# Contrast adjustment on one core: 32 KB rows in twelve equal tiles, six buffers, two hardware DMA queues, sums shared by two engines, a first tile loaded in four interleaved pieces, and instructions in program order

## The chip, the cores and the metric

The kernel runs on one core of one Trainium2 chip. The profile's names for its engines are used throughout: DVE (vector work, here the sums and the min), ACT (here the relu and, after the change, half of the sums), PE (matrix products, here to turn the sums of the rows into the images' means), POOL and SP (here they issue DMAs; POOL also writes constants). Sixteen DMA engines (so the page counts them) carry the data between main memory and the on-chip memory; a load is a DMA into the chip, a store one out of it, and each is carried as packets, here one row of a tile each (32 KB on a full tile). A row of a tile lies in one partition of the on-chip memory, a tile in 128 of them (128x8192 in the profile). A buffer is room there for one tile.

The metric is device time in microseconds (us), median of several runs; lower is better. The profile's span, from the first to the last instruction, is a little shorter than the device time: for the same run it is 1.7 to 2.1 us shorter, so differences in span and in time mean the same. Different chips were used for different sets of runs, and each set has its own runs of the kernel before. I compare within a set.

## The reference

```python
batch, c, h, w = 16, 3, 512, 512          # float32, 50.33 MB in, 50.33 MB out
mean = np.mean(x, axis=(2, 3), keepdims=True)
return np.clip(mean + factor * (x - mean), 0, 1)      # factor = 1.5
```

There are 48 images of 512 x 512. Each image needs its whole mean before any of its pixels can be written.

## The kernel before

The kernel writes `factor * x + (1 - factor) * mean`, cut off at 0 by the relu and at 1 by the min. A tile holds four images as 128 rows of 8192 numbers (32 rows per image); the last four images are two tiles of half the size.

```python
TILE_IMGS = [4] * 11 + [2, 2]
X_BUFS = 5
STORE_ENGINE = "gpsimd"
# ... cut: blockw, a block matrix of (1 - factor) / n_pix, one block per image ...
for i, N in enumerate(TILE_IMGS):
    # ... cut: tile and addresses ...
    nc.sync.dma_start(out=xt, in_=src)                     # load, SP's queue
    rsum = rpool.tile([P, 1], f32)
    nc.vector.tensor_reduce(out=rsum, in_=xt, axis=mybir.AxisListType.X, op=mybir.AluOpType.add)
    pbias = psum.tile([P, 1], f32)
    nc.tensor.matmul(pbias, blockw[N], rsum, start=True, stop=True)
    bias = bpool.tile([P, 1], f32)
    nc.scalar.copy(out=bias, in_=pbias)
    nc.scalar.activation(out=xt, in_=xt, func=mybir.ActivationFunctionType.Relu,
                         bias=bias, scale=factor)
    nc.vector.tensor_scalar(out=xt, in0=xt, scalar1=1.0, scalar2=None, op0=mybir.AluOpType.min)
    store_eng.dma_start(out=dst, in_=xt)                   # store, POOL's queue
    # ... cut ...
```

The program does not fix the order of instructions on an engine: the framework's scheduler chooses it.

Of the kernel before, what the change touches and what calls it, by code (L numbers as in the profile page):

```python
# [1 line left out]

# [4 lines left out]


TILE_IMGS = [4] * 11 + [2, 2]  # L10
X_BUFS = 5
STORE_ENGINE = "gpsimd"


@with_exitstack
def kernel(
    ctx: ExitStack,
    tc: tile.TileContext,
    x: bass.AP,
    factor: float,  # L20
    out: bass.AP,
):
    nc = tc.nc
    P = 128

    B, C, H, W = x.shape
    n_img = B * C
    n_pix = H * W

    factor = float(factor)  # L30
    f32 = mybir.dt.float32

    assert sum(TILE_IMGS) == n_img
    NMAX = max(TILE_IMGS)

    x_f = x.rearrange("b c h w -> (b c h w)")
    out_f = out.rearrange("b c h w -> (b c h w)")

    wconst = (1.0 - factor) / float(n_pix)

    consts = ctx.enter_context(tc.tile_pool(name="consts", bufs=1))
    blockw = {}
    for N in sorted(set(TILE_IMGS)):
        wt = consts.tile([P, P], f32, name=f"blockw{N}")
        PPI = P // N
        if N == 1:
            nc.gpsimd.memset(wt, wconst)
        else:
            nc.gpsimd.memset(wt, 0.0)  # L49
            for b in range(N):  # L50
                nc.gpsimd.memset(wt[b * PPI : (b + 1) * PPI, b * PPI : (b + 1) * PPI], wconst)  # L51
        blockw[N] = wt

    xpool = ctx.enter_context(tc.tile_pool(name="xpool", bufs=X_BUFS))
    rpool = ctx.enter_context(tc.tile_pool(name="rpool", bufs=12))
    bpool = ctx.enter_context(tc.tile_pool(name="bpool", bufs=12))
    psum = ctx.enter_context(tc.tile_pool(name="psum", bufs=8, space=bass.MemoryType.PSUM))

    if STORE_ENGINE == "sync":
        store_eng = nc.sync  # L60
    elif STORE_ENGINE == "act":
        store_eng = nc.scalar
    else:
        store_eng = nc.gpsimd

    pix_off = 0
    for i, N in enumerate(TILE_IMGS):
        FREE = n_pix * N // P
        npix_tile = n_pix * N

        xt = xpool.tile([P, NMAX * n_pix // P], f32, name="xt")[:, :FREE]
        src = bass.AP(tensor=x_f.tensor, offset=pix_off, ap=[[FREE, P], [1, FREE]])
        dst = bass.AP(tensor=out_f.tensor, offset=pix_off, ap=[[FREE, P], [1, FREE]])
        nc.sync.dma_start(out=xt, in_=src)  # L74

        rsum = rpool.tile([P, 1], f32)
        nc.vector.tensor_reduce(  # L77
            out=rsum,
            in_=xt,
            axis=mybir.AxisListType.X,  # L80
            op=mybir.AluOpType.add,
        )

        pbias = psum.tile([P, 1], f32)
        nc.tensor.matmul(pbias, blockw[N], rsum, start=True, stop=True)  # L85

        bias = bpool.tile([P, 1], f32)
        nc.scalar.copy(out=bias, in_=pbias)  # L88

        nc.scalar.activation(  # L90
            out=xt,
            in_=xt,
            func=mybir.ActivationFunctionType.Relu,
            bias=bias,
            scale=factor,
        )
        nc.vector.tensor_scalar(  # L97
            out=xt,
            in0=xt,
            scalar1=1.0,  # L100
            scalar2=None,
            op0=mybir.AluOpType.min,
        )
        store_eng.dma_start(out=dst, in_=xt)  # L104

        pix_off += npix_tile


# [1 line left out]
_INS = ['x', 'factor']  # L110
_OUTS = [((16, 3, 512, 512), 'float32')]
#: Inputs that are plain numbers.
_NUMBERS = {'factor': 1.5}


# [26 lines left out]
```

## Time and profile before

| | before |
|---|---|
| time, median of 3 runs | 239.89 us (239.85 to 240.51) |
| span of the profiled run | 238.6 us |
| DVE / ACT busy | 66% / 37% of the span |
| DMA slices at 90% or more | 38 of 40 |

These are lines of the page of the kernel before: busy time per engine, then the span in 40 equal slices (DMA in tenths busy, where 9 is 90% or more, and GB/s moved).

```profile
PE 7.4 (3%) x26; PEld 6.5 (3%) x26; DVE 156.5 (66%) x26; ACT 89.1 (37%) x27; POOL 10.3 (4%) x25
...
DMA  7999999999999999999999999999999999999995
GB/s 269 434 439 439 439 439 352 439 434 439 439 439 439 439 434 434 423 428 412 423 439 439 434 439 439 439 439 439 434 428 426 426 404 428 431 434 439 428 434 214
```

The row of nines is the answer to what bounds the kernel. The packets in the trace say how tight the bound is: a packet of 32 KB takes 1.213 us (median on both queues), and each of the 16 engines carries 100.66 MB / 16 / 32768 = 192 of them, so, at that packet time, 192 x 1.213 = 232.9 us of the 238.6 us cannot be saved by any ordering of this traffic. The other 5.7 us are the start, the end and a few slow packets.

The table of instruction groups, with shapes kept apart, gives the price of each step on a full tile (after the bar: busy us in total, mean ns of one; then the idle time before, and what ended it):

```profile
L77 DVE TENSOR_REDUCE rsum<-xt 128x1 f32<-128x8192 f32 x11 | 95.5, 8685 | 56.1 <-DMA xt<-in_x_dram 56.1
L90 ACT ACTIVATE xt<-xt,bias 128x8192 f32<-128x8192 f32 x11 | 78.4, 7124 | 0.4
L97 DVE TENSOR_SCALAR xt<-xt 128x8192 f32<-128x8192 f32 x11 | 48.6, 4417 | 0.0
```

Finally some lines of the timeline (start, length, engine, line, operation; in brackets the idle time before):

```profile
22.64 7.12 ACT L90 ACTIVATE xt<-xt,bias 128x8192 f32<-128x8192 f32 x1
22.73 8.69 DVE L77 TENSOR_REDUCE rsum<-xt 128x1 f32<-128x8192 f32 x1 [1.02 <-DMA xt<-in_x_dram]
31.33 4.42 DVE L97 TENSOR_SCALAR xt<-xt 128x8192 f32<-128x8192 f32 x1
...
35.66 8.68 DVE L77 TENSOR_REDUCE rsum<-xt 128x1 f32<-128x8192 f32 x1
36.06 0.67 POOL L104 DMA_DIRECT2D out_dram<-xt  x1 [34.02 <-DVE xt L97]
...
205.31 2.46 POOL L104 DMA_DIRECT2D out_dram<-xt  x1 [9.72 <-DVE xt L97]
205.36 2.29 DVE L97 TENSOR_SCALAR xt<-xt 128x4096 f32<-128x4096 f32 x1 [0.34 <-ACT xt L90]
```

DVE sums one tile (22.73) while ACT applies the bias of the one before (22.64), and takes the min of that earlier tile at 31.33. So from one sum to the next DVE needs 35.66 - 22.73 = 12.9 us when nothing is waited for, although a single tile's chain from landed load to issued store lasts 36.06 - 13.0 = 23 us. I call the first number the pitch and the second the chain. (The line at 205.31 is an exception: POOL's issue took 2.46 us instead of 0.53, ending 0.12 us after the DVE instruction that ran from 205.36 to 207.65. It cost nothing here: the packets of that store had their turn only at 216.2 us.) The DMA engines need 19.4 us per tile (2 x 8 packets of 1.213 us per engine), so they, not the pitch, set the pace.

### The profile page before, as it was taken

What the parts mean: (1) busy time and instruction counts of PE and PEld (TensorE: products, weight loads), DVE (VectorE), ACT (ScalarE), POOL (GpSimd) and SP (SyncE); (2) the same over time, 40 slices, a digit from 0 to 9 for tenths busy, and PEclk for the clock granted to TensorE, in tenths of its full rate; (3) what the DMA queues carried; (4) which work ended last, traced back from release to release, by engine and by line L of the source; (5) the groups of instructions that cost most, each with busy time, mean ns of one, the idle gap of its engine ahead of it and who ended that gap; (6) DMA issues with size and microseconds to landing.
All of it is one profiled execution on the core that took longest, in us unless ns stands there. A gap on an engine that the chain in (4) does not pass through costs nothing.

```text
span 238.6 us, 238 instructions
## 1 busy us (share of the span) xinstructions
PE 7.4 (3%) x26; PEld 6.5 (3%) x26; DVE 156.5 (66%) x26; ACT 89.1 (37%) x27; POOL 10.3 (4%) x25
## 2 busy tenths in 40 slices
PE   0000000000000000000000000000000000000000
PEld 0000000000000000000000000000000000000000
DVE  0088999999599079459629909917945979742300
ACT  2002966472906601900920650470190095406000
POOL 2000001000000000000000000000000000500000
DMA  7999999999999999999999999999999999999995
GB/s 269 434 439 439 439 439 352 439 434 439 439 439 439 439 434 434 423 428 412 423 439 439 434 439 439 439 439 439 434 428 426 426 404 428 431 434 439 428 434 214
DMA packets 3744, 100.66 MB, mean 422 GB/s; under 512 B 416, under 2 KB 416, under 8 KB 416
## 3 DMA queue, kind: packets, MB, share of 16 engines
q1 hardware_dynamic: 1872, 50.33, 49.4%
q0 software_dynamic: 1872, 50.33, 49.0%
HBM read 50.33 MB, written 50.33 MB: 422 GB/s over the span
## 4 chain that ended last, share of the span: by engine, by line
issue 38%; DMA 35%; DVE 18%; POOL 2%; POOLq 0%; SPq 0%
DMA xt<-in_x_dram 19%; DMA out_dram<-xt 16%; DVE rsum L77 11%; DVE xt L97 7%; POOL out_dram L104 2%; POOLq L137 0%; SPq L74 0%; POOLq L104 0%
## 5 line engine op out<-in xcount | busy, mean ns | idle before, releaser
L77 DVE TENSOR_REDUCE rsum<-xt 128x1 f32<-128x8192 f32 (+1 forms) x13 | 104.4, 8029 | 61.7 <-DMA xt<-in_x_dram 61.7
L90 ACT ACTIVATE xt<-xt,bias 128x8192 f32<-128x8192 f32 (+1 forms) x13 | 85.8, 6598 | 0.4
L97 DVE TENSOR_SCALAR xt<-xt 128x8192 f32<-128x8192 f32 (+1 forms) x13 | 53.2, 4091 | 5.0 <-ACT xt L90 5.0
L88 ACT COPY bias<-pbias 128x1 f32<-128x1 f32 x13 | 2.1, 160 | 130.6 <-PE pbias L85 130.6
L104 POOL DMA_DIRECT2D out_dram<-xt x13 | 9.0, 692 | 213.0 <-DVE xt L97 212.8
L85 PE MATMUL pbias<-rsum,blockw 128*128 128x1 f32 x26 | 7.4, 355 | 209.5 <-DVE rsum L77 209.5
L85 PEld LDWEIGHTS pbias<-rsum,blockw 128*128 128x128 f32 x26 | 6.5, 311 | 210.3 <-DVE rsum L77 107.1
L88 ACT ACT_TABLE_LOAD x1 | 1.3, 1283 | 0.8 <-PEq L123 0.8
L51 POOL MEMSET blockw<- 32x32 f32 (+1 forms) x6 | 0.8, 128 | 0.2
L49 POOL MEMSET blockw<- 128x128 f32 x2 | 0.3, 205 | 0.3 <-POOLq L123 0.3
L123 POOL MEMSET const-float32-0.0<- 128x1 f32 x1 | 0.1, 104 | 0.2 <-issue 0.2
L123 POOL MEMSET const-bfloat16-1.0<- 128x1 bf16 x1 | 0.1, 113 | 0.0
L123 POOL MEMSET const-uint8-127<- 128x1 uint8 x1 | 0.1, 113 | 0.0
L123 POOL MEMSET const-float32-1.0<- 128x1 f32 x1 | 0.1, 110 | 0.0
## 6 DMA issues: line engine op xcount, KB each, us to landing
xt<-in_x_dram SPq DMA_DIRECT2D x11, 4096.0 KB, 24.6
out_dram<-xt POOLq DMA_DIRECT2D x11, 4096.0 KB, 36.0
xt<-in_x_dram SPq DMA_DIRECT2D x2, 2048.0 KB, 19.5
out_dram<-xt POOLq DMA_DIRECT2D x2, 2048.0 KB, 19.1
```

The source lines that it names most:

```text
L49: nc.gpsimd.memset(wt, 0.0)
L51: nc.gpsimd.memset(wt[b * PPI : (b + 1) * PPI, b * PPI : (b + 1) * PPI], wconst)
L77: nc.vector.tensor_reduce(out=rsum, in_=xt, axis=mybir.AxisListType.X, op=mybir.AluOpType.add,)
L85: nc.tensor.matmul(pbias, blockw[N], rsum, start=True, stop=True)
L88: nc.scalar.copy(out=bias, in_=pbias)
L90: nc.scalar.activation(out=xt, in_=xt, func=mybir.ActivationFunctionType.Relu, bias=bias, scale=factor,)
L97: nc.vector.tensor_scalar(out=xt, in0=xt, scalar1=1.0, scalar2=None, op0=mybir.AluOpType.min,)
L104: store_eng.dma_start(out=dst, in_=xt)
L123: nc = _bacc.Bacc("TRN2", target_bir_lowering=False, num_devices=1)
```

## The change

The intent: rows of 32 KB in every tile, a shorter chain (sums shared by DVE and ACT, relu and min in four overlapping quarters), more buffers, stores from ACT's hardware queue in place of POOL's software queue (hardware_dynamic and software_dynamic on the pages), and an earlier start by loading the first tile in four pieces. The whole diff rewrites the file; this is its core.

```diff
-TILE_IMGS = [4] * 11 + [2, 2]
-X_BUFS = 5
-STORE_ENGINE = "gpsimd"
+P, ROW, BUFS, CHUNK, HALF, JUNK, SPLIT = 128, 8192, 6, 2048, ROW // 2, 2048, 4   # (one per line)
 ...
+    def load(t):
+        xt = xpool.tile([P, ROW], f32, name="xt")
+        if t == 0:
+            for r in range(SPLIT):
+                src = bass.AP(tensor=x_f.tensor, offset=r * ROW,
+                              ap=[[SPLIT * ROW, P // SPLIT], [1, ROW]])
+                nc.sync.dma_start(out=xt[r::SPLIT, :], in_=src)
+        else:
+            nc.sync.dma_start(out=xt, in_=dram(x_f, t))
 ...
+    def compute(t):
-        nc.vector.tensor_reduce(out=rsum, in_=xt, ...)
+        nc.vector.tensor_reduce(out=sums[:, 0:1], in_=xt[:, 0:HALF], ...)
+        for j in range(n_act):                         # (ROW - HALF) // JUNK = 2
+            nc.scalar.activation(out=junk, in_=xt[:, a : a + JUNK], func=Act.Copy,
+                                 accum_out=sums[:, 1 + j : 2 + j])
-        nc.tensor.matmul(pbias, blockw[N], rsum, start=True, stop=True)
+        for j in range(1 + n_act):
+            nc.tensor.matmul(pbias, blockw, sums[:, j : j + 1], start=j == 0, stop=j == n_act)
         nc.scalar.copy(out=bias, in_=pbias)
+        for c in range(0, ROW, CHUNK):
+            nc.scalar.activation(out=part, in_=part, func=Act.Relu, bias=bias, scale=factor)
+            nc.vector.tensor_scalar(out=part, in0=part, scalar1=1.0, scalar2=None, op0=Alu.min)
-        store_eng.dma_start(out=dst, in_=xt)           # gpsimd
+        nc.scalar.dma_start(out=dram(out_f, t), in_=tiles.pop(t))
 ...
+    with tc.manual_schedule():                         # instructions stay in program order
+        for t in range(min(BUFS, n_tiles)):
+            load(t)
+        for t in range(n_tiles):
+            compute(t); store(t)
+            if t + BUFS < n_tiles:
+                load(t + BUFS)
```

(Lines are joined, some are left out, and remarks after # are added for print.) The last block takes the order of instructions out of the scheduler's hands.

More of the change, by code (lines that the diff above doesn't have):

```diff
@@ L5 @@
 import concourse.tile as tile
-from concourse import bass_utils, mybir
+from concourse import mybir
 from concourse._compat import with_exitstack
-TILE_IMGS = [4] * 11 + [2, 2]
-X_BUFS = 5
-STORE_ENGINE = "gpsimd"
+P = 128
+ROW = 8192
+BUFS = 6
+CHUNK = 2048
+HALF = ROW // 2
+JUNK = 2048
+SPLIT = 4
 @with_exitstack
@@ L23 @@
     nc = tc.nc
-    P = 128
+    f32 = mybir.dt.float32
+    Alu = mybir.AluOpType
+    Act = mybir.ActivationFunctionType
     B, C, H, W = x.shape
-    n_img = B * C
-    n_pix = H * W
+    n_img, n_pix = B * C, H * W
+    ppi = n_pix // ROW
+    per_tile = P // ppi
+    n_tiles = n_img // per_tile
+    assert ppi * ROW == n_pix and per_tile * n_tiles == n_img
     factor = float(factor)
-    f32 = mybir.dt.float32
-    assert sum(TILE_IMGS) == n_img
-    NMAX = max(TILE_IMGS)
+    wconst = (1.0 - factor) / float(n_pix)
@@ L36, with dram @@
     x_f = x.rearrange("b c h w -> (b c h w)")
     out_f = out.rearrange("b c h w -> (b c h w)")
-    wconst = (1.0 - factor) / float(n_pix)
+    def dram(ap, t):
+        return bass.AP(tensor=ap.tensor, offset=t * P * ROW, ap=[[ROW, P], [1, ROW]])
     consts = ctx.enter_context(tc.tile_pool(name="consts", bufs=1))
-    blockw = {}
-    for N in sorted(set(TILE_IMGS)):
-        wt = consts.tile([P, P], f32, name=f"blockw{N}")
-        PPI = P // N
-        if N == 1:
-            nc.gpsimd.memset(wt, wconst)
-        else:
-            nc.gpsimd.memset(wt, 0.0)
-            for b in range(N):
-                nc.gpsimd.memset(wt[b * PPI : (b + 1) * PPI, b * PPI : (b + 1) * PPI], wconst)
-        blockw[N] = wt
@@ L54 @@
-    xpool = ctx.enter_context(tc.tile_pool(name="xpool", bufs=X_BUFS))
-    rpool = ctx.enter_context(tc.tile_pool(name="rpool", bufs=12))
-    bpool = ctx.enter_context(tc.tile_pool(name="bpool", bufs=12))
-    psum = ctx.enter_context(tc.tile_pool(name="psum", bufs=8, space=bass.MemoryType.PSUM))
-    if STORE_ENGINE == "sync":
-        store_eng = nc.sync
-    elif STORE_ENGINE == "act":
-        store_eng = nc.scalar
-    else:
-        store_eng = nc.gpsimd
-    pix_off = 0
-    for i, N in enumerate(TILE_IMGS):
-        FREE = n_pix * N // P
-        npix_tile = n_pix * N
-        xt = xpool.tile([P, NMAX * n_pix // P], f32, name="xt")[:, :FREE]
-        src = bass.AP(tensor=x_f.tensor, offset=pix_off, ap=[[FREE, P], [1, FREE]])
-        dst = bass.AP(tensor=out_f.tensor, offset=pix_off, ap=[[FREE, P], [1, FREE]])
-        nc.sync.dma_start(out=xt, in_=src)
-        rsum = rpool.tile([P, 1], f32)
+    xpool = ctx.enter_context(tc.tile_pool(name="xpool", bufs=BUFS))
@@ new lines @@
+    jpool = ctx.enter_context(tc.tile_pool(name="jpool", bufs=1))
+    rpool = ctx.enter_context(tc.tile_pool(name="rpool", bufs=2))
+    bpool = ctx.enter_context(tc.tile_pool(name="bpool", bufs=2))
+    psum = ctx.enter_context(tc.tile_pool(name="psum", bufs=2, space=bass.MemoryType.PSUM))
+    blockw = consts.tile([P, P], f32, name="blockw")
+    nc.gpsimd.memset(blockw, 0.0)
+    for a in range(0, P, ppi):
+        nc.gpsimd.memset(blockw[a : a + ppi, a : a + ppi], wconst)
+    tiles = {}
+    def load(t):
+        xt = xpool.tile([P, ROW], f32, name="xt")
+        if t == 0:
+            for r in range(SPLIT):
+                src = bass.AP(
+                    tensor=x_f.tensor, offset=r * ROW, ap=[[SPLIT * ROW, P // SPLIT], [1, ROW]]
+                )
+                nc.sync.dma_start(out=xt[r::SPLIT, :], in_=src)
+        else:
+            nc.sync.dma_start(out=xt, in_=dram(x_f, t))
+        tiles[t] = xt
@@ L77 @@
+    def compute(t):
+        xt = tiles[t]
+        n_act = (ROW - HALF) // JUNK
+        sums = rpool.tile([P, 1 + n_act], f32, name="sums")
         nc.vector.tensor_reduce(
-            out=rsum,
-            in_=xt,
-            axis=mybir.AxisListType.X,
-            op=mybir.AluOpType.add,
-        )
-        pbias = psum.tile([P, 1], f32)
-        nc.tensor.matmul(pbias, blockw[N], rsum, start=True, stop=True)
-        bias = bpool.tile([P, 1], f32)
-        nc.scalar.copy(out=bias, in_=pbias)
@@ L90 @@
-        nc.scalar.activation(
-            out=xt,
-            in_=xt,
-            func=mybir.ActivationFunctionType.Relu,
-            bias=bias,
-            scale=factor,
-        )
-        nc.vector.tensor_scalar(
-            out=xt,
-            in0=xt,
-            scalar1=1.0,
-            scalar2=None,
-            op0=mybir.AluOpType.min,
-        )
-        store_eng.dma_start(out=dst, in_=xt)
-        pix_off += npix_tile
+            out=sums[:, 0:1], in_=xt[:, 0:HALF], axis=mybir.AxisListType.X, op=Alu.add
+        )
@@ new lines, in compute @@
+        for j in range(n_act):
+            junk = jpool.tile([P, JUNK], f32, name="junk")
+            a = HALF + j * JUNK
+            nc.scalar.activation(
+                out=junk, in_=xt[:, a : a + JUNK], func=Act.Copy, accum_out=sums[:, 1 + j : 2 + j]
+            )
+        pbias = psum.tile([P, 1], f32, name="pbias")
+        for j in range(1 + n_act):
+            nc.tensor.matmul(pbias, blockw, sums[:, j : j + 1], start=j == 0, stop=j == n_act)
+        bias = bpool.tile([P, 1], f32, name="bias")
@@ new lines, in compute, with store @@
+        nc.scalar.copy(out=bias, in_=pbias)
+        for c in range(0, ROW, CHUNK):
+            part = xt[:, c : c + CHUNK]
+            nc.scalar.activation(out=part, in_=part, func=Act.Relu, bias=bias, scale=factor)
+            nc.vector.tensor_scalar(out=part, in0=part, scalar1=1.0, scalar2=None, op0=Alu.min)
+    def store(t):
+        nc.scalar.dma_start(out=dram(out_f, t), in_=tiles.pop(t))
[3 more added lines that the diff above has]
+        for t in range(n_tiles):
+            compute(t)
+            store(t)
+            if t + BUFS < n_tiles:
+                load(t + BUFS)
```

## The prediction

> **What bounds it now.** The 16 DMA engines, from start to end. The page's slices show them 90% busy or more in 38 of 40 slices, at 439 GB/s in most. In the trace, a 32 KB packet takes 1.213 us (median of both queues). Each engine carries 100.66 MB / 16 = 192 such packets: 192 x 1.213 = 232.9 us of the 238.6 us span. The other 5.7 us: 1.75 us until the first packet; about 0.9 us of first packets at 1.4 to 2.2 us and staggered starts; about 0.65 us extra on load packets when the first store begins (35 to 40 us); 0.6 us of unequal engine ends; 1.8 us from the last packet to the end. DVE is 66% busy, ACT 37%; in the table of groups DVE idles 56 us for loads. The load cadence in the timeline is 19.4 us per 4 MB tile, load plus store (2 x 8 x 1.213): compute paces nothing later.
>
> **What changes.** Eleven of 13 tiles had 32 KB rows already.
> - Sums: a DVE reduce of 128x8192 takes 8.69 us; halved, about 4.4 us, beside ACT's 4096 elements (3.7 us as one, perhaps 4.1 as two). Relu and min in four chunks overlap: about 8 us (7.12 + 0.8 overhead) plus one 1.2 us min, instead of 7.12 + 4.42 with DVE waits. Load to store issue on the first tile falls from 23 us (13.0 to 36.1) to about 16.5 us; compute still fits 19.4.
> - The first store starts some 7 us earlier, while loads fill the engines anyway: no gain. Six buffers: loads never starved; no gain.
> - Stores from ACT's queue, not POOL's: [...] both queues' medians are 1.213 us. Gain: perhaps the 0.65 us bump.
> - Tail: the two half tiles go. Loads alone run before the first store for about T = 9.7 + 16.5 us; after the last load the same 26 us of stores remain, and the last tile needs 16.5 us before its 9.7 us store. It just fits, without slack (before: some 14 us by this count), so engine skew can expose 0 to 2 us.
> - First tile as four DMAs of 32 rows: may trim 0.3 us of start skew. [...]
>
> **Sum.** 239.9 - 0.65 - 0.3 + 0.7 tail gives 239.6; I take 239.5 us[...]: 237.6 to 243.0. Faster by over 2% would need under 235.1: 0.03. Within 2%: 0.85. Slower: 0.12.
>
> **What would show it.** Right: packets at 1.213 us in the middle; DMA full until the last slices; DVE share near 45%, ACT near 60%; load cadence 19.4 us; first store near 28 us. Tail step: a gap in DMA between the last two stores of under 2 us. [...]
>
> **What would make it wrong.** [...] ACT, which now works in order, issuing late enough for a dry store queue at the end; a slower accumulating activation; a packet time that changes with two hardware queues.

Passages marked as cut, here and in the expectations below, gave or rested on rules of the hardware that no trace or run of this case shows. No term of the sum is cut: 239.9 - 0.65 - 0.3 + 0.7 comes to about 239.6, taken as 239.5 us. What is cut, besides a rule about queues, is a risk named for the first tile in four pieces; it had no term of its own and stood only in the range, 237.6 to 243.0.

## The result and the profile after

| set of runs | kernel | median | ratio to before of the same set, 95% interval |
|---|---|---|---|
| first | after, 4 runs | 241.0 us (240.49 to 241.04) | 1.0043, 1.0025 to 1.0061 |
| first | before, 4 runs | 239.87 us | |
| second, another chip | after, 6 runs | 240.15 us (240.14 to 240.67) | 1.0003, 0.9983 to 1.0024 |
| second | before, 11 runs | 240.41 us | |

A ratio is the mean time of one kernel's fast runs over that of the other's fast runs of the same rounds, so not quite the ratio of the medians quoted. Executions over 1.5% slower than the fastest of the same kernel are left out of the means. The first set has after 0.4% slower, the second has them equal. I conclude that the change gains nothing, to within about 0.6 per cent (the wider end of the first interval), and explain no part of the 0.4%.

The same lines of the page of the kernel after:

```profile
PE 17.2 (7%) x72; PEld 16.3 (7%) x72; DVE 111.7 (47%) x60; ACT 143.4 (60%) x109; POOL 0.9 (0%) x9
...
DMA  7999999999999999999999999999999999999995
GB/s 263 438 438 438 438 351 438 438 433 416 422 433 433 427 438 418 438 433 438 438 411 427 438 438 438 433 438 422 433 434 438 438 433 427 433 438 438 422 422 219
```

The row of DMA is the same row of nines, and the sum of the bytes is the same to 0.02 MB. DVE fell from 156.5 to 111.7 us and ACT rose from 89.1 to 143.4 us, without any effect on the rate. The table of groups of after:

```profile
L97 ACT ACTIVATE xt<-xt,bias 128x2048 f32<-128x2048 f32 x48 | 92.2, 1990 | 0.4
L98 DVE TENSOR_SCALAR xt<-xt 128x2048 f32<-128x2048 f32 x48 | 58.9, 1227 | 69.1 <-ACT xt L97 69.1
...
L87 ACT ACTIVATE junk<-xt 128x2048 f32<-128x2048 f32 x24 | 45.8, 1910 | 46.8 <-DMA xt<-in_x_dram 41.4 <-DVE xt L98 5.1
...
L81 DVE TENSOR_REDUCE sums<-xt 128x1 f32<-128x4096 f32 x12 | 53.0, 4418 | 43.6 <-DMA xt<-in_x_dram 43.6
```

DVE's sum halved from 8.69 to 4.42 us, ACT's two pieces cost 1.91 us each (and 0.19 to read out each sum), and a quarter of the relu costs 1.99 us where a quarter of 7.12 us would be 1.78. These are close to the costs that I had estimated (4.4, 4.1 for both pieces, and 8 us for four quarters). The timeline of after (ACTq is ACT's sequencer issuing a store):

```profile
13.34 4.42 DVE L81 TENSOR_REDUCE sums<-xt 128x1 f32<-128x4096 f32 x1 [13.34 <-DMA xt<-in_x_dram]
...
27.26 1.23 DVE L98 TENSOR_SCALAR xt<-xt 128x2048 f32<-128x2048 f32 x1 [0.67 <-ACT xt L97]
28.40 4.41 DVE L81 TENSOR_REDUCE sums<-xt 128x1 f32<-128x4096 f32 x1
28.52 0.37 ACTq L101 DMA_DIRECT2D out_dram<-xt  x1
...
73.67 4.42 DVE L81 TENSOR_REDUCE sums<-xt 128x1 f32<-128x4096 f32 x1 [0.23 <-DMA xt<-in_x_dram]
...
209.28 4.42 DVE L81 TENSOR_REDUCE sums<-xt 128x1 f32<-128x4096 f32 x1 [4.26 <-DMA xt<-in_x_dram]
...
224.39 0.34 ACTq L101 DMA_DIRECT2D out_dram<-xt  x1
```

The chain is 28.52 - 13.3 = 15.2 us where it was 23, and the pitch 28.40 - 13.34 = 15.1 us where it was 12.9. So the change shortened the chain and lengthened the pitch: in program order DVE sums the next tile (28.40) only after the last min of this one (27.26 + 1.23). From 73.67 on, each tile waits for its load, as before. At the end, the last store is issued at 224.39; its first packets start at 226.40, when the packets of the store ahead are through, and the trace shows no gap.

### The profile page after: what moved, and what is told of

It reads as the page before. It is cut to its first block, busy times and chain, and to the rows that moved or that the text cites. A ratio compares the mean times of both kernels' runs of the same rounds, so it can differ in the third digit from the quotient of the medians.

```text
span 239.2 us, 437 instructions
## 1 busy us (share of the span) xinstructions
PE 17.2 (7%) x72; PEld 16.3 (7%) x72; DVE 111.7 (47%) x60; ACT 143.4 (60%) x109; POOL 0.9 (0%) x9
## 4 chain that ended last, share of the span: by engine, by line
ACT 38%; DVE 27%; another core or an unknown queue 12%; PE 7%; DMA 4%; issue 3%; SPq 1%; DVEq 0%
ACT xt L97 37%; DVE sums L81 22%; PE pbias L92 7%; DVE xt L98 5%; DMA xt<-in_x_dram 4%; ACT bias L94 1%; SPq L72 1%; DVEq L81 0%
## 5 line engine op out<-in xcount | busy, mean ns | idle before, releaser
L97 ACT ACTIVATE xt<-xt,bias 128x2048 f32<-128x2048 f32 x48 | 92.2, 1990 | 0.4
L98 DVE TENSOR_SCALAR xt<-xt 128x2048 f32<-128x2048 f32 x48 | 58.9, 1227 | 69.1 <-ACT xt L97 69.1
L87 ACT ACTIVATE junk<-xt 128x2048 f32<-128x2048 f32 x24 | 45.8, 1910 | 46.8 <-DMA xt<-in_x_dram 41.4
L81 DVE TENSOR_REDUCE sums<-xt 128x1 f32<-128x4096 f32 x12 | 53.0, 4418 | 43.6 <-DMA xt<-in_x_dram 43.6
L92 PE MATMUL pbias<-sums,blockw 128*128 128x1 f32 x72 | 17.2, 355 | 197.9 <-DVE sums L81 197.9
L92 PEld LDWEIGHTS pbias<-sums,blockw 128*128 128x128 f32 x72 | 16.3, 326 | 198.9 <-DVE sums L81 181.0
L87 ACT ACT_TABLE_LOAD x1 | 1.3, 1283 | 13.3 <-DMA xt<-in_x_dram 13.3
L87 ACT ACTIVATION_READ_ACCUMULATOR junk<-xt 128x1 f32 x24 | 4.5, 186 | 0.0
L61 POOL MEMSET blockw<- 32x32 f32 x4 | 0.5, 118 | 0.2
```

What stands on the lines that cost most here:

```text
L61: nc.gpsimd.memset(blockw[a : a + ppi, a : a + ppi], wconst)
L81: nc.vector.tensor_reduce(out=sums[:, 0:1], in_=xt[:, 0:HALF], axis=mybir.AxisListType.X, op=Alu.add)
L87: nc.scalar.activation(out=junk, in_=xt[:, a : a + JUNK], func=Act.Copy, accum_out=sums[:, 1 + j : 2 + j])
L92: nc.tensor.matmul(pbias, blockw, sums[:, j : j + 1], start=j == 0, stop=j == n_act)
L97: nc.scalar.activation(out=part, in_=part, func=Act.Relu, bias=bias, scale=factor)
L98: nc.vector.tensor_scalar(out=part, in0=part, scalar1=1.0, scalar2=None, op0=Alu.min)
```

## The experiments

Where the text says "the packets", it means the single DMA packets in the trace (start, length, queue, size). Runs e0 to e3 share one chip, e5 to e8 another, and e4 and e9 to e11 a third. The kernel before ran on each; the control e0 ran on the first alone, so where e4 to e11 are set beside the control's trace, two chips are compared.

### e0_after_again: the control

The kernel after, unchanged.

> The kernel after, unchanged, as the control beside which the other three of this set are read. Both theories: 1.003 to 1.006 of the kernel before, that is 240.6 to 241.3 us, first packet near 2.07 us, last packet near 237.7 us, and time minus span near 1.8 us where the kernel before has about 1.25.

Measured: 240.15 us, 1.0003 (0.9983 to 1.0024) of before, lower than either theory put it. First packet 2.06 us, last packet's end 236.9 us. Time minus span was 1.74 to 1.84 us for after, but 1.91 to 2.06 us for before on this chip, not 1.25. My 1.25 came from setting a span of one chip's run against the median of others; the "0.5 us outside the span" never existed. That idea falls.

### e1_unsplit: the first tile in one DMA

```diff
-SPLIT = 4
+SPLIT = 1
```

> The kernel after with its first tile in one DMA. Theory A (the split only delays the first packet, because the issue of 32 strided rows takes 0.54 us where 128 rows took 0.37): first packet back at about 1.75 us, spread of the first sixteen packets back to about 1 us, time 0.2 to 0.4 us below the control. Rival B (the split helps by starting the engines together, as it was meant to): time 0.2 us or more above the control. Rival C [...]: the first tile's data end falls from 12.9 us by more than a microsecond; the trace of after already speaks against this.

Measured: 240.39 us, 1.0016 (0.9983 to 1.0048), against 1.0003 for the control. Half of theory A is in the trace: the first packet comes at 1.73 us instead of 2.06. The issue of a DMA of 32 rows four apart took SP 0.54 us in the trace of after, that of 128 rows 0.37 us in before, which accounts for 0.17 of these 0.33 us. But the first sixteen packets start within 0.48 us of each other, not the 1 us that A expected, and the gain that A forecast does not reach the end: the last packet ends at 236.95 us in this trace and at 236.92 in the control's. The time is no lower either: the median is 0.24 us above the control's, which would suit B, but this kernel's fast runs scatter from 239.89 to 242.04 us. The four pieces neither help nor hurt measurably. C is excluded too: the first tile's data end at 12.8 us here and 13.0 us in the control.

### e2_contig: the four pieces made of neighbouring rows

```diff
-tensor=x_f.tensor, offset=r * ROW, ap=[[SPLIT * ROW, P // SPLIT], [1, ROW]]
+tensor=x_f.tensor, offset=r * (P // SPLIT) * ROW, ap=[[ROW, P // SPLIT], [1, ROW]]
-nc.sync.dma_start(out=xt[r::SPLIT, :], in_=src)
+nc.sync.dma_start(out=xt[r * (P // SPLIT) : (r + 1) * (P // SPLIT), :], in_=src)
```

> The first tile as four DMAs of 32 neighbouring rows each. [...] packets of the first tile take about twice 1.213 us and the tile's data end near 20 us instead of 12.9, time some 5 to 7 us above the control. [...]

Measured: 249.38 us, 1.0381 (1.0356 to 1.0407), 9.2 us above the control, more than the 5 to 7 expected. In stretches of 5 us (the last two columns of this view are the busy share of the DMA engines and the GB/s) the kernel after loads its first tile so:

```profile
2.00:7.00 5.00, 0.00 (x0) 0.00 (x0) 0.00 (x0) 0.00 (x0) 0.00 (x0) 1.00 1.12 419
7.00:12.00 5.00, 0.00 (x0) 0.00 (x0) 0.00 (x0) 0.00 (x0) 0.00 (x0) 1.00 0.97 419
```

and this kernel so:

```profile
2.00:7.00 5.00, 0.00 (x0) 0.00 (x0) 0.00 (x0) 0.00 (x0) 0.00 (x0) 1.00 1.02 216
7.00:12.00 5.00, 0.00 (x0) 0.00 (x0) 0.00 (x0) 0.00 (x0) 0.00 (x0) 1.00 0.94 197
...
17.00:22.00 5.00, 0.00 (x0) 0.00 (x0) 0.00 (x0) 0.00 (x0) 0.00 (x0) 1.00 0.92 203
```

The engines are as busy as ever, but move half: the packets of the first tile take 2.4 to 2.6 us, about twice 1.213 as forecast, and its data end at 22.5 us instead of 13. That is 197 to 216 GB/s against 419. The edit changed both the partitions that a piece fills and the addresses of main memory that it reads, and no run separates the two, but the packets speak for the partitions: the sixteen first packets of the third piece, where the rows pass from partition 63 to 64, took 2.38 us each, while those of the second and the fourth took 2.54 to 2.57 like the other packets after the first round; in main memory the addresses run on alike at all three borders. Why the packets slow is not shown. But pieces of neighbouring rows cost 9.2 us here, and "every fourth row" in the change avoids it: 32 rows four apart run at 1.213 us per packet (median) after the first round. It is a precaution against the cost of splitting, not a gain over not splitting (e1).

### e3_before_act: the kernel before, stores issued by ACT

```diff
-STORE_ENGINE = "gpsimd"
+STORE_ENGINE = "act"
```

> The kernel before with nothing changed but the engine that issues its stores: ACT instead of POOL. Theory A (the 0.5 us by which time minus span grew comes with the second hardware queue, or with leaving POOL's): time minus span about 1.8 us and the span within 0.5 us of before, so 0.3 to 0.8 us above before. Rival (that part belongs to something else in the new kernel): time minus span stays at 1.25 us and the time within 0.3 us of before. ACT waits for DVE before each store, but has 19 us per tile for some 8 us of work, so the load cadence stays 19.4 us.

Measured: 271.91 us, 1.1316 (1.1289 to 1.1342). Both theories missed by 30 us. (Time minus span was 1.86 to 1.96 us, so it did not fall to the 1.8 of after.) This is ACT's timeline:

```profile
35.69 13.27 ACTq L104 DMA_DIRECT2D out_dram<-xt  x2
49.00 0.16 ACT L88 COPY bias<-pbias 128x1 f32<-128x1 f32 x1 [9.68 <-DVE xt L97]
57.86 0.16 ACT L88 COPY bias<-pbias 128x1 f32<-128x1 f32 x1 [8.70 <-PE pbias L85]
57.93 14.14 ACT L90 ACTIVATE xt<-xt,bias 128x8192 f32<-128x8192 f32 x2
```

The scheduler put two store issues in a row on ACT, the second of which waits for a min that DVE does only after another sum; the bias of the next tile, ready at 44.9 us (its matmul ran from 44.31 to 44.90), is copied at 49.00, and the relu after it comes still later. DMA engines stand idle for 32.5 us in the sum over the run, averaged over the engines, against 4.3 us in the control. I had counted ACT's work and not the places at which its stores would stand in its queue. The run does not say whether the hardware queue itself costs anything; e4 and e10 do.

### e4_after_pool: the kernel after, stores issued by POOL

```diff
-nc.scalar.dma_start(out=dram(out_f, t), in_=tiles.pop(t))
+nc.gpsimd.dma_start(out=dram(out_f, t), in_=tiles.pop(t))
```

> The kernel after with its stores issued by POOL, as before had them, everything else kept. Theory (the kind of queue is neutral, and the loss in the run of before with ACT's stores came from the order in which ACT's instructions were then put): the same as after within 0.5 us, 0.997 to 1.006 of before; ACT no longer waits 1.7 us per tile for DVE's last min, so the pitch may fall by up to that, which gains nothing. Rival (hardware queues are faster): 1 us or more above after.

Measured: 240.94 us, 1.0041 (1.0026 to 1.0055), within the expectation. The kind of queue is neutral to about half a per cent here. This agrees with the packets of before and after: the median is 1.213 us on SP's, POOL's and ACT's queue alike. The pitch stayed at 28.54 - 13.48 = 15.1 us; the fall that I had thought possible did not come. The run also settles a term of my sum: load packets are slow where the first store comes in, by 0.88 us per engine here, 0.82 in the control, 0.69 in before, and 0.66 in the run without any computing below. Neither the kind of queue nor the computing makes this loss. It is not there at every first meeting of stores and loads either: in e2 it is only 0.02 us, and in all other runs 0.61 to 0.93. Why e2 was spared is open.

### e5_no_share: sums on DVE alone

```diff
-HALF = ROW // 2
+HALF = ROW
```

> The kernel after with its shared sums undone: DVE reduces all 8192 columns of every tile (8.69 us by the trace of before) and ACT none. Each tile's chain from landed load to issued store grows from 15.2 us by 4.3 for the longer reduce, less 0.9 for two matmul pairs fewer: about 18.6 us. Theory (the chain of the first tile only lengthens the stretch in which loads have the engines alone, and the same stretch of stores then covers the chain of the last tile, so a chain that is equally long on all tiles costs nothing): same as after within 0.4 us, so 0.998 to 1.005 of before. Rival (the last tile's chain is exposed): 3.4 us longer, near 1.014.

Measured: 249.03 us, 1.0379 (1.0359 to 1.0398). Both theories missed: 9 us, not 0 and not 3.4. The timeline of DVE shows why:

```profile
13.40 8.69 DVE L81 TENSOR_REDUCE sums<-xt 128x1 f32<-128x8192 f32 x1 [13.40 <-DMA xt<-in_x_dram]
...
31.90 8.68 DVE L81 TENSOR_REDUCE sums<-xt 128x1 f32<-128x8192 f32 x1
...
216.51 8.68 DVE L81 TENSOR_REDUCE sums<-xt 128x1 f32<-128x8192 f32 x1
```

No sum after the first waits for a load: the bracket with the idle time is missing on all of them. The kernel is paced by its own pitch, (216.51 - 31.90) / 10 = 18.46 us, from first to last tile: 13.40 + 12 x 18.46 = 234.9, and the last store was issued at 235.09. A pitch of 18.5 us is under the 19.4 us that the engines need per tile, which is why I thought it free. But the first loads land 9.7 us apart, while they have the engines alone, so the loads start with a lead of some tiles; at 0.9 us per tile the computing never works it off, and the engines run dry at the end:

```profile
222.00:227.00 5.00, 0.56 (x2) 0.50 (x2) 3.19 (x1) 1.04 (x2) 0.00 (x0) 1.00 0.97 419
227.00:232.00 5.00, 0.00 (x0) 0.00 (x0) 2.51 (x3) 5.00 (x4) 0.00 (x0) 1.00 0.00 0
```

DMA falls to nothing between 227 and 232 us. So the shared sums are not decoration: under program order they are what keeps the kernel from losing 9 us.

### e6_last_slow and e7_both_slow: a longer chain on the last tile, or on first and last

```diff
+SLOW = (11,)          # e7_both_slow: (0, 11)
 ...
+        if t in SLOW:
+            for _ in range(4):
+                pad = jpool.tile([P, JUNK], f32, name="junk")
+                nc.scalar.activation(out=pad, in_=xt[:, 0:JUNK], func=Act.Copy)
         bias = bpool.tile([P, 1], f32, name="bias")
```

> The kernel after with four idle copies on ACT (1.9 us each) put before the bias of the last tile alone. ACT has about 2 us of waiting there, so the last store is issued about 5.7 us later, near 230.1 us. In the trace of after the last store was issued at 224.4 and its first packets began at 226.4 to 227.6, just when the packets of the store ahead were through; a fresh store needs about 1 us from issue to first packet, so the slack is 1 to 2 us. Theory: a gap of 3.5 to 4.7 us of idle DMA near 227 to 231 us and a time 3.5 to 4.7 us above after (1.015 to 1.021 of before). Rival (plenty of stores are still queued): no change. Rival (no slack at all): plus 5.7 us.

> The same four copies on the first tile as well as on the last. Theory: the first store starts some 6.9 us later, loads run ahead by that much, and the stores left over at the end cover the slow last tile: no gap, same as after within 0.4 us, though more work was added than in the run with the slow last tile alone, which it beats by 3.5 us or more. Rival (each delay of a chain costs by itself): at least as long as the run with the slow last tile alone.

Measured: 244.17 us, 1.0175 (1.0154 to 1.0196) with the slow last tile; 240.11 us, 1.0005 (0.999 to 1.0021) with the slow first tile added. More work made it 4.1 us faster, as the theory had it, and no rival did. The windows at the end of the run with the slow last tile alone, and its last sum and last store:

```profile
222.00:227.00 5.00, 0.00 (x0) 0.00 (x0) 2.45 (x2) 5.00 (x3) 0.00 (x0) 1.00 0.81 347
227.00:232.00 5.00, 0.00 (x0) 0.00 (x0) 2.45 (x2) 2.21 (x2) 0.00 (x0) 1.00 0.24 105
```

```profile
209.72 4.42 DVE L82 TENSOR_REDUCE sums<-xt 128x1 f32<-128x4096 f32 x1 [4.26 <-DMA xt<-in_x_dram]
...
230.51 0.34 ACTq L106 DMA_DIRECT2D out_dram<-xt  x1
```

and of the run with both, with its first store:

```profile
222.00:227.00 5.00, 0.00 (x0) 0.00 (x0) 1.17 (x1) 0.00 (x0) 0.00 (x0) 1.00 0.97 419
227.00:232.00 5.00, 0.00 (x0) 0.00 (x0) 0.00 (x0) 0.00 (x0) 0.00 (x0) 1.00 0.99 426
```

```profile
35.50 0.38 ACTq L106 DMA_DIRECT2D out_dram<-xt  x1
```

In the first, the chain from the last sum to the last store is 230.51 - 209.72 = 20.8 us, 5.7 longer than 15.1, and a gap opens (24% busy); the store's first packet starts 0.84 us after its issue (231.35), where about 1 us was expected. In the second, the first store is issued at 35.50 us instead of 28.6, loads run ahead by those 6.9 us, and the stores left over at the end cover the slow tile. Of the 5.7 us, 244.17 - 240.11 = 4.1 us reached the time (the same comes out against the control: 1.0175 less 1.0003, times 240). The slack of the kernel after is thus 5.7 - 4.1 = 1.6 us, between the 1 and 2 us expected.

### e8_bufs3: three buffers

```diff
-BUFS = 6
+BUFS = 3
```

> The kernel after with three buffers instead of six. A buffer's cycle is a load at half rate (19.4 us), 1.6 us to the landing seen by ACT, a chain of 15.2 us, a wait and a store at half rate (19.4 us), and about 2.7 us until the next load's packets: some 58 us or more over three buffers, 19.4 us each, so three just miss feeding the engines. My estimate by a fluid model of two queues: about 12 us of idle DMA, near 251 us (1.05). Rival (buffers were a limit at six or five already): the loss would be in proportion much larger, since four and five would already starve; rival (buffers play no part): same as after.

Measured: 257.93 us, 1.0749 (1.0705 to 1.0793). The direction is right, the size 7 us short. Idle time of the engines is 13.8 us, 9.5 more than in the control, against my estimate of 12; the rest is in longer packets: packet time per engine is 241.4 us instead of 234.8, some four fifths of the growth on loads (1.284 us mean, 1.229 in the control). My fluid model had no such term. (For the two delays that it assumed, 1.6 and 2.7 us, the traces show: 1.66 us from the last packet of the last load to its first use on ACT in after, 207.55 to 209.21; and in before 1.67 us from the last packet of the first store to the issue of the next load, 59.77 to 61.44, and 1.00 us from the first load's issue to its first packet, 0.75 to 1.75.) Four and five buffers were not run, so "six buffers give no gain over five" rests on the traces of before and after, whose DMA engines are not idle in the middle of the run.

### e9_threequarter: DVE sums three quarters

```diff
-HALF = ROW // 2
+HALF = 3 * ROW // 4
```

> The kernel after with DVE summing 6144 of the 8192 columns instead of 4096 (or of 8192, in the run without shared sums). Its pitch, from one tile's start on DVE to the next's when nothing is waited for, should lie between 15.0 and 18.5 us, at about 16.8. Theory (a kernel in program order loses time only when first start plus 12 pitches passes the moment at which the last store's turn comes: 13.4 + 12 x 16.8 = 215 against 225 us; 18.5 gave 235): no loss, the same as after within 0.4 us, 0.998 to 1.005 of before. Rival (any lengthening of every tile's chain costs in proportion, as the run without shared sums alone might suggest): about half of its 9 us, near 1.02.

Measured: 243.87 us, 1.016 (1.0145 to 1.0175): the theory missed, and the rival's 1.02 is nearer. The timeline of DVE:

```profile
13.45 6.55 DVE L81 TENSOR_REDUCE sums<-xt 128x1 f32<-128x6144 f32 x1 [13.45 <-DMA xt<-in_x_dram]
...
30.21 6.55 DVE L81 TENSOR_REDUCE sums<-xt 128x1 f32<-128x6144 f32 x1
...
113.72 6.55 DVE L81 TENSOR_REDUCE sums<-xt 128x1 f32<-128x6144 f32 x1
...
131.91 6.55 DVE L81 TENSOR_REDUCE sums<-xt 128x1 f32<-128x6144 f32 x1 [1.41 <-DMA xt<-in_x_dram]
```

The part of the theory about the pitch holds: it is 16.7 us, and from 131.91 on DVE waits for loads again, so the lead was worked off. Yet the last store is issued at 227.72 us, 3.3 later than in after: the last sum starts 1.6 us later (210.90 against 209.28), and the chain from it to the store is 1.7 us longer. Two things show in the packets. Packet time per engine is 236.7 us, 1.85 more than in the control, on loads that take 1.3 to 2.5 us in the first few microseconds of a transfer, at each transfer from about 70 us on; and the engines drift apart: the last load ends on its first engine at 205.5 us and on its last at 209.3 (205.8 and 206.8 in the control). The last tile waits for the slowest engine while the others run dry: idle time grew by 1.9 us. The two together are the 3.75 us by which the spans differ (242.1 against 238.4); this is a sum of where the time lies, and not its cause. The chip alone does not explain it: in e4, on the same chip, packet time is 235.0 us and the last load ends on its engines between 205.8 and 206.6. Why these loads were slow is open. It is not a matter of load alone: with the longer pitch of e5 packet time was 234.6 us, as in the control. Nor can I say that it scales with the pitch.

### e10_before_order: the kernel before in program order

```diff
+    with tc.manual_schedule():
     pix_off = 0
     for i, N in enumerate(TILE_IMGS):     # ... the loop, indented, otherwise untouched
```

> The kernel before, stores on POOL as they were, with only its instructions left in program order, as the kernel after has them. DVE then can't sum the next tile while ACT works on this one: pitch 8.69 + 0.9 + 7.12 + 4.42, about 21.1 us per tile, over the 19.4 us that the engines need for a tile. Theory: 13.0 + 11 x 21.1 + 2 x 11.3 = 267.7 us to the last store's issue, plus 1.5, a 4.9 us store and the end: a span near 276 us, time 276 to 280 (1.15 to 1.17 of before). Rival (program order is harmless, and what hurt in the run with ACT's queue was the queue): same as before within 1%.

Measured: 277.49 us, 1.1562 (1.1545 to 1.1579), inside 276 to 280. The timeline of DVE:

```profile
12.99 8.69 DVE L78 TENSOR_REDUCE rsum<-xt 128x1 f32<-128x8192 f32 x1 [12.99 <-DMA xt<-in_x_dram]
...
34.11 8.68 DVE L78 TENSOR_REDUCE rsum<-xt 128x1 f32<-128x8192 f32 x1
...
256.04 4.41 DVE L78 TENSOR_REDUCE rsum<-xt 128x1 f32<-128x4096 f32 x1
```

The pitch is 34.11 - 12.99 = 21.1 us and after the last sum, at 256.04, the last store was issued at 267.71 us, where 267.7 had been worked out. With 4.9 us for a half tile's store (8 packets of 0.611 us in before) and 1.8 us from the last packet to the end (in before), the span of 275.6 us leaves, as an estimate, 1.2 us from that issue to the first packet, where 1.5 had been put. The queue was POOL's, so order alone costs 37 us in this kernel.

### e11_copy_only: the transfers by themselves

```diff
         for t in range(n_tiles):
-            compute(t)
             store(t)
```

> The kernel after with all computing taken out, so that it stores what it loads; the result is wrong on purpose. It measures what the same 24 transfers on the two hardware queues cost by themselves. Theory (DMA alone sets the time of after): 192 packets of 1.213 us, 2.1 us before the first, about 1.4 us after the last, about 1 us of slow first packets: a span of 237 to 238.5 us, the same as after within 0.7 us. Rival (computing still costs something by its waits): 2 us or more below after.

Measured: 239.44 us, 0.998 (0.9965 to 0.9994) of before; the result is wrong (it stores the input). The slices of its page:

```profile
DMA  7999999999999999999999999999999999999996
GB/s 265 442 353 441 442 441 442 441 430 419 408 419 442 441 442 442 441 442 441 430 408 414 425 441 442 442 441 442 442 436 436 403 403 441 442 442 441 442 442 265
```

With nothing to compute, the transfers of after take 0.5 us less than the kernel before (0.1 to 0.8 by the interval). As long as these transfers are kept, that is all that a change to the computing can gain.

## Why the prediction was right or wrong

**The total was right.** Forecast 239.5 us (237.6 to 243.0), "within 2%" at 0.85; measured 241.0 and, on another chip, 240.15. It is right because the bound that it rests on is right. The three corrections in the sum (-0.65, -0.3, +0.7) were all wrong, as shown below; that they nearly cancel is luck, though left out they would have moved the forecast only to 239.9.

**"The 16 DMA engines, from start to end": right, and shown.** The transfers alone take 239.44 us (e11). DVE lost 45 us of work and ACT gained 54; neither moved the time.

**Where the expected gain went.** A chain shorter by 8 us (15.2 from 23; I had forecast 16.5) is off the critical path. What the first tile saves in its chain is lost as lead of the loads, and is needed back at the last tile. e6 and e7 show both sides: 5.7 us more on the last tile cost 4.1, and 6.9 us more on the first tile as well took the 4.1 away again. The forecast "just fits, without slack" with 0 to 2 us exposed was close: the slack is 1.6 us and nothing was exposed, so the 0.7 us that I added for it was wrong.

**"Compute still fits 19.4": right for this kernel, but the reason was incomplete.** To fit under the engines' 19.4 us is not enough. e5 has a pitch of 18.5 us and loses 9 us, because the loads' lead from the start must be worked off within twelve tiles. And e9, at 16.7 us, loses 3.7 us although it works the lead off. The kernel after is nearer to a loss than I thought.

**What I did not see: the order.** I treated shared sums and quarters as pure saving. In fact the change gives up the scheduler's overlap of neighbouring tiles (pitch 12.9 us) and buys a short chain in its place (pitch 15.1 us). In the kernel before, order alone costs 37 us (e10), and ACT's store queue in the scheduler's order 31 us (e3). That before and after are equal is two sound designs meeting the same bound, not a change too small to matter. The kernel after in the scheduler's order was not run.

**"Gain: perhaps the 0.65 us bump": wrong.** The slow loads at the first store come with either kind of queue, and without computing (e4, e11).

**"May trim 0.3 us of start skew": no gain.** The first sixteen packets start no closer together that could be told: within 0.39 to 1.00 us of each other in the nine traces with four interleaved pieces, and within 0.48 (e1), 0.64 (e3), 1.04 (before) and 1.06 (e10) with the first tile in one DMA. The first one comes 0.3 us later, and e1 sees no difference in time. **The risk of splitting** did not strike this split, but e2 paid 9.2 us for pieces of neighbouring rows; why is not shown.

**Open:** why loads were slow in e8 and e9; why the first store in e2 did not slow them; and whether the 0.4% of the first set is anything, since the second has 0.0%.

## What to carry to other kernels

Before shortening computation in a kernel whose DMA row is all nines, run its transfers alone: that one run bounds the gain while the transfers stay as they are, here 0.5 us. If instructions are kept in program order, look at the pitch as well as the chain: the pitch must be far enough under the transfer time per tile to work off the lead that the first loads get, and the last tile's chain must fit into the stores left over. e5 and e6 show what missing either costs; e9 worked the lead off and still lost 3.7 us, for a reason that stays open. If a load is cut into pieces by rows, interleave them: here that kept the packets at 1.213 us, where neighbouring rows took 2.4 to 2.6 (e2).

## What else the traces show

- A part of a tile made of every fourth row: 1.213 us (median after the first round) per 32 KB packet in after. A part made of neighbouring rows: 2.4 to 2.6 us (e2).
- From the start of the issuing instruction, which itself lasts 0.34 to 0.37 us, to a store's first packet, on ACT's hardware queue: 0.84 us with idle engines (230.51 to 231.35 in e6), but 4.1 us (28.52 to 32.66 in after) when the engines were full of loads.
- In after, the first tile's use starts 0.43 us after its last packet's end (12.88 to 13.31), with no stores about; the last tile's 1.66 us after (207.55 to 209.21), with stores under way. No run tested whether the stores make the difference.
- The loss when the first store meets a stream of loads: 0.61 to 0.93 us per engine in thirteen of the fourteen traces, with or without computing (e11), and 0.02 in e2.
